# Column chunk 0 of each weight unit ahead of chunk 1, second halves evicted behind the Strassen products, third units gathered

## The chip, the cores and the metric

The kernel runs on one core of a Trainium2 chip. The metric is the device time of one execution in microseconds; the time before is 2516.99 us, the median of three runs (2516.59 to 2519.99). What can be told from no change in this kernel is about 0.2%, or 5 us.

## The reference

Two layers of a decoder trunk, float32, 256 positions, model width 2048. What matters here is which products there are and in which order they depend on one another:

```
for l in range(2):
    h = rms_norm(x, mix_norm[l]);  proj = h @ w_in[l]                # q, k, v, u/v of the SGU, two sets of gate logits
    branch_a = attention(q, k, v) @ w_attn_branch[l]                 # window 128, rotary, sinks
    branch_b = chunked_sgu(gelu(uv)) @ w_sgu_branch[l]
    merged = sigmoid(gates_a) * branch_a + sigmoid(gates_b) * branch_b
    x = x + merged @ w_out[l]
    h2 = rms_norm(x, ffn_norm[l])
    x = x + (silu(h2 @ w_gate[l]) * (h2 @ w_up[l])) @ w_down[l]      # hidden width 5632
```

## The kernel before

**Jobs, units, parts.** Every weight product is a list of *jobs* (`add_job`). A job makes 1024 output columns, two *chunks* of 512 (c = 0 and 1), for both tiles of 128 positions (t = 0 and 1): four PSUM banks. There are five banks (`banks`), so a job starts with the one bank that the job before didn't use. The contraction runs over *units* of 512 rows. A unit comes in two loads of 256 rows (h = 0 and 1, 1 MB each, on SyncE's queue, four raw buffers), and each load holds two *parts* of 256 rows and 512 columns. A part is 12 matmuls: two tiles, two blocks of 128 rows, and three products, because each operand is split into a high and a low half (`three`, lines 320 to 322).

**The stream.** The parts of all jobs form one list. `Stream.fill` runs a few parts ahead of TensorE: ScalarE writes a part's high half (`high`, line 223, six buffers), VectorE its low half (`low`, line 231, five buffers). VectorE makes a low half when TensorE has released the buffer five parts earlier. While TensorE works at part n, VectorE makes the low half of part n+4, ScalarE the high half of part n+5, and VectorE the weight sum of part n+6 if it needs one (`add`, line 215).

**Strassen.** In 42 jobs the first unit goes through seven products of 6 matmuls instead of four parts (`PRODUCTS`: 11, t1, t2, 22, t3, 21, t4). Four of the seven need a weight sum (t1, t2, t3, t4). Between them ScalarE copies banks: after 11 into x, after t1 into `p5` and after t2 into `u2` (`kept`, line 345), after t3 into y (line 365). Product 22 writes the bank that `p5` was copied from, t3 the one that `u2` was copied from, t4 the bank y. After t4, VectorE adds `u2` and `p5` into the two banks of chunk 1 (lines 367 and 368). These are all jobs from the second set of gates on: two gate halves (gate0, gate1), two w_out halves, and in the FFN, which runs in three rounds of 4, 4 and 3 blocks of 512 hidden columns, the gate and up jobs and the two down halves of each round. A gate half is followed by the matching w_sgu_branch half (sgu0, sgu1), which has two units and no Strassen. In the third round the last hidden block is one job whose two chunks are gate and up.

**The order of the other work** is written by hand, by each engine's program order. `soon(fn)` issues fn in the next step, behind that step's `fill`. `after(n, fn)` issues it n *slots* later; a part is one slot, a Strassen product half a slot. When a chunk's last part is issued, `done(c, ps)` is called:

- gate jobs: tanh on ScalarE at once (lines 959, 1002), both tiles; on VectorE, `gated` (line 1007) by `soon`.
- up jobs: `upped` (line 1016) by `soon`, both tiles; one slot later the block is transposed.
- branch jobs: `gated` and `merge` (lines 968 and 981) by `soon`; one slot later the transposition.
- w_out and down: the residual add (line 915) by `soon`; where a norm follows, one slot later the transposition and two later the squares on ScalarE (line 533).

**Transposition** (`transposed`) makes a chunk into a unit for a later job. Either two VectorE block transposes (line 414), sixteen small DMAs that GpSimd issues (line 419, `gathered`), then ScalarE's high half (line 462) and VectorE's low half (line 469) when 5 slots or more have gone by; or (`on_pe`) eight transposes on TensorE (line 483) with the halves read from PSUM. The third unit of four (o = 2, or `f == fs[2]`) goes by TensorE, the others by the gather.

Before, the parts of a unit run (h, c) = (0,0), (0,1), (1,0), (1,1). Chunk 0 so ends one part before its job, and its eviction falls into the job's last part; chunk 1's falls into the next job's first step, and its transposition one slot, that is two products, later.

Of the kernel before, what the change touches and what calls it, by code (L numbers as in the profile page):

```python
# [11 lines left out]
ALU = mybir.AluOpType  # L12
AX = mybir.AxisListType

P = 128
NT = 2
# [11 lines left out]
CW = 512  # L28
NCH = D // CW
# [6 lines left out]
N_LOW = 5  # L36
N_BIG = 24
G_BUSY, G_LAND = 3.5, 1.5
Q_FIRST = 15
Q_STEP = 4  # L40
LOAD_BY = (1, 2, 3, 4)
ROUNDS = ((0, 1, 2, 3), (4, 5, 6, 7), (8, 9, 10))
M_OUT, M_FFN, M_DOWN = 1, 1, 1
# [6 lines left out]
def hybrid_trunk(ctx: ExitStack, tc: tile.TileContext, x, mix_norm, w_in, q_norm, k_norm, sinks,  # L50
# [56 lines left out]
    def add_job(cols, units=None, m=0):  # L107
        job = Job(cols, units, m)
        jobs.append(job)
        held = {}  # L110
        for u in job.units[:m]:
            held[u] = load_of(job, u, 0), load_of(job, u, 1)
        for i, name in enumerate(PRODUCTS if m else ()):
            for n, u in enumerate(job.units[:m]):
                a, b = held[u]
                v = {"11": (a, 0), "12": (a, 1), "21": (b, 0), "22": (b, 1), "new": (f"sum{len(jobs)}_{u}", 0)}
                dst, one, two = {"11": ("11", 0, 0), "22": ("22", 0, 0), "21": ("21", 0, 0),
                                 "t1": ("new", "12", "11"), "t2": ("11", "22", "new"),
                                 "t3": ("12", "22", "12"), "t4": ("new", "21", "11")}[name]
# [776 lines left out]
    def residual(units, nxt, sums, out_at=None):  # L896

        for j in range(0, NCH, 2):

            def done(c, ps, j=j):  # L900
                o = j + c
                soon(lambda: added(o, ps))
                if nxt is not None:
                    after(2 if o == 2 else 1, lambda: nxt.unit(o, on_pe=o == 2, sums=sums and o == 0))
                    after(2, lambda: nxt.squares(o))
                    if o == NCH - 1:
                        after(4, lambda: nxt.finish())

            def added(o, ps):
                for t in range(NT):  # L910
                    n = 2 if out_at is not None and o == NCH - 1 else 1
                    w = CW // n
                    for i in range(n):
                        sl = slice(o * CW + i * w, o * CW + (i + 1) * w)
                        nc.vector.tensor_tensor(out=xs[:, t, sl], in0=ps[t][:, i * w:(i + 1) * w], in1=xs[:, t, sl],  # L915
                                                op=ALU.add)
                        if out_at is not None:
                            eng = nc.sync if i == 0 else nc.scalar
                            eng.dma_start(out_at[0, t * P:(t + 1) * P, sl], xs[:, t, sl])
            run(units, done)  # L920

    prepare(0)
# [1 line left out]
    for l in range(DEPTH):  # L924

        pl = layer[l]
        parameters(pl)
        kv = slot([P, NT, CW], name="kv")
        qs = [slot([P, NT, CW], name="q") for _ in range(2)]
        att, spa = Attention(pl), Spatial(pl, norm)  # L930

        def scaled_into(dst, ps):
            for t in range(NT):
                nc.vector.tensor_scalar(out=dst[:, t, :], in0=ps[t], scalar1=norm.r[t], scalar2=None, op0=ALU.mult)

# [12 lines left out]
        for done in (kv_done, q_done)[::-1 if l else 1]:  # L948
            run(norm.units, done)
        run(norm.units, spa.v)  # L950
        run(norm.units, spa.u)

        ga, gb, mT = [None] * NCH, [None] * NCH, [None] * NCH

        def gate(dst, j):
            def done(c, ps):
                dst[j + c] = slot([P, NT, CW], name="gate")
                for t in range(NT):
                    nc.scalar.activation(dst[j + c][:, t, :], ps[t], AF.Tanh, scale=norm.rh[t])
            run(norm.units, done)  # L960

        def branch(dst, j, units, then=None):
            def done(c, ps):
                d = dst[j + c]

                def gated():
                    for t in range(NT):
                        nc.vector.scalar_tensor_tensor(out=d[:, t, :], in0=d[:, t, :], scalar=1.0, in1=ps[t],
                                                       op0=ALU.add, op1=ALU.mult)
                        if then is not None:  # L970
                            then(j + c, t)

                soon(gated)
                if then is not None:
                    after(2 if j + c == 2 else 1,
                          lambda: transposed(mT, j + c, ga[j + c], scale=0.5, on_pe=j + c == 2,
                                                sums=M_OUT and j + c == 0))
            run(units, done)

        def merge(j, t):  # L980
            nc.vector.tensor_tensor(out=ga[j][:, t, :], in0=ga[j][:, t, :], in1=gb[j][:, t, :], op=ALU.add)

        for j in (0, 2):
            gate(ga, j)
        after(2, lambda nrm=norm: nrm.add_sums(0))
        for j in (0, 2):
            branch(ga, j, att.attT)
        for j in (0, 2):
            gate(gb, j)
            branch(gb, j, spa.sguT, merge)  # L990

        norm = Norm(ffn_cols(l))
        residual(mT, norm, M_FFN)

        nxt = Norm(mix_cols(l + 1)) if l + 1 < DEPTH else None
        for i, fs in enumerate(ROUNDS):
            hid, hT = {}, {}

            def gate_done(f, ps):
                hid[f] = a = slot([P, NT, CW], name="hid")  # L1000
                for t in range(NT):
                    nc.scalar.activation(a[:, t, :], ps[t], AF.Tanh, scale=norm.rh[t])

                def gated():
                    for t in range(NT):
                        th = a[:, t, :]
                        nc.vector.scalar_tensor_tensor(out=th, in0=th, scalar=1.0, in1=ps[t], op0=ALU.add, op1=ALU.mult)

                soon(gated)

            def up_done(f, ps):
                a = hid[f]

                def upped():
                    for t in range(NT):
                        nc.vector.scalar_tensor_tensor(out=a[:, t, :], in0=ps[t], scalar=norm.rr[t], in1=a[:, t, :],
                                                       op0=ALU.mult, op1=ALU.mult)

                soon(upped)
                after(2 if f == fs[2] else 1, lambda: transposed(hT, f, a, on_pe=f == fs[2], sums=f in fs[:M_DOWN]))  # L1020

            for f in fs[::2]:
                if f + 1 < NF:
                    run(norm.units, lambda c, ps: gate_done(f + c, ps))
                    run(norm.units, lambda c, ps: up_done(f + c, ps))
                else:
                    run(norm.units, lambda c, ps: (gate_done, up_done)[c](f, ps))
# [44 lines left out]
```

## Time and profile before

| | |
|---|---|
| median of 3 runs | 2516.99 us |
| the profiled execution | 2519.38 us, its span 2517.7 us |
| TensorE busy | 2481.6 us (99%), 11102 matmuls |
| VectorE busy | 1900.4 us (75%) |
| ScalarE busy | 1344.8 us (53%) |
| GpSimd busy | 465.0 us (18%) |
| HBM read | 475.27 MB |

A row of the groups names line, engine and operation, what is written from what, the count, then busy time and the mean ns of one, then the engine's idle time before it and who ended it. A row of the timeline is start, length, engine and line. A wait row is who waited for whom, the total in us, how often, and the longest. PEld is TensorE's weight load, which runs ahead of the matmul that it belongs to. The ends of matmuls are modelled and overlap, so a stall of TensorE is read from start to start.

### The profile page before, as it was taken

How to read it: one execution, taken by the hardware profiler on the slowest of the kernel's cores; microseconds unless marked ns; L12 is line 12 of the kernel's file. 1: busy time of each engine (PE TensorE's matmuls, PEld its weight loads, DVE VectorE, ACT ScalarE, POOL GpSimd, SP SyncE). 2: the span in 40 equal slices, each digit the busy share in tenths (PEclk: the TensorE clock that was granted, in tenths of full speed). 3: DMA queues.
4: the chain of work that ended last, by engine and by line, in shares of the span. 5: the costliest groups of instructions: out<-in, count | busy, mean ns of one | idle time of the engine just before them, and what ended most of it. 6: DMA issues, size and time to landing. Idle time of an engine off the chain costs nothing. (4 is left out here: it accounts for less than half of the span.)

```text
span 2517.7 us, 30567 instructions
## 1 busy us (share of the span) xinstructions
PE 2481.6 (99%) x11102; PEld 2031.9 (81%) x11102; DVE 1900.4 (75%) x2183; ACT 1344.8 (53%) x1658; POOL 465.0 (18%) x767
## 2 busy tenths in 40 slices
PE   9999999999999999999999999999999999999999
PEld 7888887778888888888788888877788888788887
DVE  6796667787877787777868956678878776877686
ACT  5455455465554555555654544554656455645554
POOL 1512302131210021003225022021402100210020
PEclk9999999999999999999999999999999999999999
DMA  7745656656565656566666456565756656665654
GB/s 267 232 156 164 205 200 201 192 188 221 181 229 168 233 184 219 191 217 202 217 211 216 155 166 215 193 202 165 227 199 214 208 186 209 197 209 184 223 179 164
DMA packets 157271, 502.99 MB, mean 200 GB/s; under 512 B 19712, under 2 KB 22368, under 8 KB 157120
## 3 DMA queue, kind: packets, MB, share of 16 engines
q1 hardware_dynamic: 133408, 476.87, 56.9%
q0 software_dynamic: 23392, 23.89, 3.6%
q8 instruction: 87, 1.43, 0.2%
q14 instruction: 64, 0.52, 0.1%
q10 hardware_dynamic: 320, 0.27, 0.0%
HBM read 475.27 MB, written 2.10 MB: 190 GB/s over the span
## 5 line engine op out<-in xcount | busy, mean ns | idle before, releaser
L231 DVE TENSOR_TENSOR wlo<-raw,whi 128x1024 fp32r<-128x1024 f32 (+1 forms) x940 | 1131.7, 1219 | 489.9 <-PE acc L321 401.1
L223 ACT ACTIVATE whi<-raw 128x1024 fp32r<-128x1024 f32 (+1 forms) x940 | 978.6, 1058 | 824.2 <-PE acc L322 789.9
L320 PE MATMUL acc<-whi,uh 128*128 128x512 f32 x3164 | 1240.9, 392 | 7.9 <-DVE acc L367 3.6
L321 PE MATMUL acc<-wlo,uh 128*128 128x512 f32 x3164 | 1233.0, 390 | 3.0 <-DVE wlo L231 3.0
L322 PE MATMUL acc<-whi,ul 128*128 128x512 f32 x3164 | 1233.0, 390 | 0.0
L320 PEld LDWEIGHTS acc<-whi,uh 128*128 128x128 f32 x3164 | 594.5, 188 | 139.1 <-DVE acc L367 7.4
L321 PEld LDWEIGHTS acc<-wlo,uh 128*128 128x128 f32 x3164 | 594.8, 188 | 125.2 <-DVE wlo L231 3.9
L322 PEld LDWEIGHTS acc<-whi,ul 128*128 128x128 f32 x3164 | 594.6, 188 | 125.1
L419 POOL DMA_DIRECT2D tt<-blk x624 | 359.4, 583 | 1749.0 <-ACT whi L223 725.5
L320 PE MATMUL acc<-whi,sh 128*128 128x512 f32 x336 | 139.2, 414 | 19.1 <-ACT p L345 11.0
L223 ACT ACTIVATE whi<-sum 128x1024 fp32r<-128x1024 f32 x84 | 89.3, 1063 | 101.8 <-PE acc L322 58.0
L321 PE MATMUL acc<-wlo,sh 128*128 128x512 f32 x336 | 132.0, 393 | 0.0
L322 PE MATMUL acc<-whi,sl 128*128 128x512 f32 x336 | 131.9, 393 | 0.0
L231 DVE TENSOR_TENSOR wlo<-sum,whi 128x1024 fp32r<-128x1024 f32 x84 | 101.8, 1212 | 8.4 <-PE acc L321 8.4
L320 PEld LDWEIGHTS acc<-whi,sh 128*128 128x128 f32 x336 | 63.4, 189 | 52.2 <-ACT p L345 23.3
L322 PEld LDWEIGHTS acc<-whi,sl 128*128 128x128 f32 x336 | 63.4, 189 | 14.1
L469 DVE SCALAR_TENSOR_TENSOR ul<-tt,uh 128x512 fp32r<-128x512 f32 x44 | 28.4, 687 | 58.3 <-ACT uh L462 58.3
L321 PEld LDWEIGHTS acc<-wlo,sh 128*128 128x128 f32 x336 | 63.6, 189 | 10.3
L462 ACT ACTIVATE uh<-tt 128x1024 fp32r<-128x1024 f32 x22 | 23.2, 1057 | 81.1 <-DMA tt<-blk 81.1
L215 DVE TENSOR_TENSOR raw<-raw,sum 128x1024 f32<-128x1024 f32 x42 | 51.4, 1225 | 1.4
L215 DVE TENSOR_TENSOR sum<-raw 128x1024 f32<-128x1024 f32 x42 | 51.2, 1219 | 0.0
L215 DVE TENSOR_TENSOR raw<-raw,raw 128x1024 f32<-128x1024 f32 x42 | 51.2, 1218 | 0.0
(144 smaller groups left out, 1144.9 us busy)
## 6 DMA issues: line engine op xcount, KB each, us to landing
raw<-in_w_in_dram SPq DMA_DIRECT2D x112, 1024.0 KB, 5.0
raw<-in_w_down_dram SPq DMA_DIRECT2D x88, 1024.0 KB, 5.9
raw<-in_w_gate_dram SPq DMA_DIRECT2D x80, 1024.0 KB, 5.4
raw<-in_w_up_dram SPq DMA_DIRECT2D x80, 1024.0 KB, 5.2
raw<-in_w_out_dram SPq DMA_DIRECT2D x32, 1024.0 KB, 6.1
tt<-blk POOLq DMA_DIRECT2D x624, 32.0 KB, 5.2
raw<-in_w_attn_branch_dram SPq DMA_DIRECT2D x16, 1024.0 KB, 5.6
raw<-in_w_sgu_branch_dram SPq DMA_DIRECT2D x16, 1024.0 KB, 5.3
```

What stands on the lines that cost most here:

```text
L215: nc.vector.tensor_tensor(out=self.raw(dst), in0=self.raw(total[0]), in1=self.raw(total[1]), op=ALU.subtract)
L223: nc.scalar.activation(hi[:, k, :], raw[:, k, :], AF.Copy)
L231: nc.vector.tensor_tensor(out=lo[:, k, :], in0=raw[:, k, :], in1=hi[:, k, :].bitcast(F32), op=ALU.subtract)
L320: nc.tensor.matmul(ps, a, hi, start=first, stop=False, skip_group_check=True)
L321: nc.tensor.matmul(ps, a, lo, start=False, stop=False, skip_group_check=True)
L322: nc.tensor.matmul(ps, b, hi, start=False, stop=last, skip_group_check=True)
L419: nc.gpsimd.dma_start(ov[j * B:(j + 1) * B, i], blk[i * B:(i + 1) * B, j].rearrange("p k t c -> p (k t) c"))
L462: nc.scalar.activation(unit.hi[:, k0 + k:k0 + k + step, :], src_t[:, k:k + step, :], AF.Copy, scale=scaled(k0 + k))
L469: nc.vector.scalar_tensor_tensor(out=flat(unit.lo[:, kk, :]), in0=flat(src_t[:, k:k + step, :]), scalar=scaled(k0 + k), in1=flat(unit.hi[: ...
```

## The change

1. In jobs with two chunks, each unit without Strassen asks for both its loads first, and its parts run (h, c) = (0,0), (1,0), (0,1), (1,1). Chunk 0 so ends two parts before its job.
2. `evicting(c, fn, then, ahead)` sets when a chunk is evicted. Chunk 0, and everything in the last job: both tiles by `soon`, `then` one slot later. Chunk 1: tile 0 by `soon`; tile 1 three slots later if the next job begins with Strassen, else one; `then` four slots later, or else two. ScalarE's tanh (`ahead`) of chunk 1 runs at once for tile 0 and one slot before tile 1's eviction for tile 1.
3. `then` holds the merge (one instruction over both tiles, where there were two), the transposition, the residual's squares, and a slot behind them the norm's `finish`.
4. Third units go through the gather. Only the last hidden block (`f == NF - 1`) is still transposed on TensorE.

```diff
             else:
-                for h in range(2):
-                    a = load_of(job, u, h)
-                    for c in range(2):
-                        parts.append(((a, c), None, a))
+                ab = [load_of(job, u, h) for h in range(2)]
+                for c in range(2):
+                    for h in range(2):
+                        parts.append(((ab[h], c), None, ab[h]))
                         job.steps.append(("whole", u, (h, c)))
...
+T1_LATE, THEN_LATE = 3, 4
+    def behind(whole, strassen):
+        return strassen if job_no[0] < len(jobs) and jobs[job_no[0]].m else whole
+
+    def evicting(c, fn, then=None, ahead=None):
+        if c == 0 or job_no[0] == len(jobs):
+            for t in range(NT):
+                if ahead is not None:
+                    ahead(t)
+                soon(lambda t=t: fn(t))
+            if then is not None:
+                after(1, then)
+        else:
+            late = behind(1, T1_LATE)
+            if ahead is not None:
+                ahead(0)
+                after(late - 1, lambda: ahead(1))
+            soon(lambda: fn(0))
+            after(late, lambda: fn(1))
+            if then is not None:
+                after(behind(2, THEN_LATE), then)
...
 residual:
-                soon(lambda: added(o, ps))
-                if nxt is not None:
-                    after(2 if o == 2 else 1, lambda: nxt.unit(o, on_pe=o == 2, sums=sums and o == 0))
-                    after(2, lambda: nxt.squares(o))
+                def then():
+                    nxt.unit(o, sums=sums and o == 0)
+                    nxt.squares(o)
                     if o == NCH - 1:
-                        after(4, lambda: nxt.finish())
+                        after(1, lambda: nxt.finish())
+                evicting(c, lambda t: added(o, t, ps), then if nxt is not None else None)
...
 gate:
+                evicting(c, lambda t: None, ahead=tanh)
 branch:
+                def then_():
+                    then(j + c)
+                    transposed(mT, j + c, ga[j + c], scale=0.5, sums=M_OUT and j + c == 0)
+                evicting(c, lambda t: nc.vector.scalar_tensor_tensor(...),
+                         then_ if then is not None else None)
...
-        def merge(j, t):
-            nc.vector.tensor_tensor(out=ga[j][:, t, :], in0=ga[j][:, t, :], in1=gb[j][:, t, :], op=ALU.add)
+        def merge(j):
+            nc.vector.tensor_tensor(out=flat(ga[j]), in0=flat(ga[j]), in1=flat(gb[j]), op=ALU.add)
...
 FFN:
+                evicting(c, gated, ahead=tanh)
-                soon(upped)
-                after(2 if f == fs[2] else 1, lambda: transposed(hT, f, a, on_pe=f == fs[2], sums=f in fs[:M_DOWN]))
+                evicting(c, upped, lambda: transposed(hT, f, a, on_pe=f == NF - 1, sums=f in fs[:M_DOWN]))
```

More of the change, by code (lines that the diff above doesn't have):

```diff
@@ L901, in done, with added @@
                 o = j + c
-                soon(lambda: added(o, ps))
-                if nxt is not None:
-                    after(2 if o == 2 else 1, lambda: nxt.unit(o, on_pe=o == 2, sums=sums and o == 0))
-                    after(2, lambda: nxt.squares(o))
+                def then():
+                    nxt.unit(o, sums=sums and o == 0)
+                    nxt.squares(o)
                     if o == NCH - 1:
-                        after(4, lambda: nxt.finish())
[L909 to L919, printed above, removed]
+                        after(1, lambda: nxt.finish())
+                evicting(c, lambda t: added(o, t, ps), then if nxt is not None else None)
+            def added(o, t, ps):
+                n = 2 if out_at is not None and o == NCH - 1 else 1
+                w = CW // n
+                for i in range(n):
+                    sl = slice(o * CW + i * w, o * CW + (i + 1) * w)
+                    nc.vector.tensor_tensor(out=xs[:, t, sl], in0=ps[t][:, i * w:(i + 1) * w], in1=xs[:, t, sl],
+                                            op=ALU.add)
+                    if out_at is not None:
+                        eng = nc.sync if i == 0 else nc.scalar
+                        eng.dma_start(out_at[0, t * P:(t + 1) * P, sl], xs[:, t, sl])
             run(units, done)
@@ L957, in done, with tanh @@
                 dst[j + c] = slot([P, NT, CW], name="gate")
-                for t in range(NT):
+                def tanh(t):
                     nc.scalar.activation(dst[j + c][:, t, :], ps[t], AF.Tanh, scale=norm.rh[t])
+                evicting(c, lambda t: None, ahead=tanh)
             run(norm.units, done)
@@ L964, in done @@
                 d = dst[j + c]
[L966 to L977, printed above, removed]
+                def then_():
+                    then(j + c)
+                    transposed(mT, j + c, ga[j + c], scale=0.5, sums=M_OUT and j + c == 0)
+                evicting(c, lambda t: nc.vector.scalar_tensor_tensor(out=d[:, t, :], in0=d[:, t, :], scalar=1.0,
+                                                                     in1=ps[t], op0=ALU.add, op1=ALU.mult),
+                         then_ if then is not None else None)
             run(units, done)
-        def merge(j, t):
-            nc.vector.tensor_tensor(out=ga[j][:, t, :], in0=ga[j][:, t, :], in1=gb[j][:, t, :], op=ALU.add)
+        def merge(j):
+            nc.vector.tensor_tensor(out=flat(ga[j]), in0=flat(ga[j]), in1=flat(gb[j]), op=ALU.add)
         for j in (0, 2):
@@ L997, in hybrid_trunk, with gate_done, tanh, gated @@
             hid, hT = {}, {}
-            def gate_done(f, ps):
+            def gate_done(f, c, ps):
                 hid[f] = a = slot([P, NT, CW], name="hid")
-                for t in range(NT):
+                def tanh(t):
                     nc.scalar.activation(a[:, t, :], ps[t], AF.Tanh, scale=norm.rh[t])
[L1004 to L1011, printed above, removed]
-                a = hid[f]
[L1014 to L1017, printed above, removed]
-                soon(upped)
-                after(2 if f == fs[2] else 1, lambda: transposed(hT, f, a, on_pe=f == fs[2], sums=f in fs[:M_DOWN]))
+                def gated(t):
+                    th = a[:, t, :]
+                    nc.vector.scalar_tensor_tensor(out=th, in0=th, scalar=1.0, in1=ps[t], op0=ALU.add, op1=ALU.mult)
+                evicting(c, gated, ahead=tanh)
+            def up_done(f, c, ps):
+                a = hid[f]
+                def upped(t):
+                    nc.vector.scalar_tensor_tensor(out=a[:, t, :], in0=ps[t], scalar=norm.rr[t], in1=a[:, t, :],
+                                                   op0=ALU.mult, op1=ALU.mult)
+                evicting(c, upped, lambda: transposed(hT, f, a, on_pe=f == NF - 1, sums=f in fs[:M_DOWN]))
             for f in fs[::2]:
                 if f + 1 < NF:
-                    run(norm.units, lambda c, ps: gate_done(f + c, ps))
-                    run(norm.units, lambda c, ps: up_done(f + c, ps))
+                    run(norm.units, lambda c, ps: gate_done(f + c, c, ps))
+                    run(norm.units, lambda c, ps: up_done(f + c, c, ps))
                 else:
-                    run(norm.units, lambda c, ps: (gate_done, up_done)[c](f, ps))
+                    run(norm.units, lambda c, ps: (gate_done, up_done)[c](f, c, ps))
             if i == len(ROUNDS) - 1:
```

## The prediction

> **What bounds the kernel now.** I read the page first, then TensorE's waits, then the timeline of one place where TensorE stands.
>
> ```profile
> span 2517.7 us, 30567 instructions
> ...
> PE 2481.6 (99%) x11102; PEld 2031.9 (81%) x11102; DVE 1900.4 (75%) x2183; ACT 1344.8 (53%) x1658; POOL 465.0 (18%) x767
> ```
>
> TensorE is the bound. Work taken from it counts in full; otherwise only its stalls can be won. The weight loads' waits name them:
>
> ```profile
> PEld acc L320 <- ACT p L345: 23.3, 36, 2.5
> PEld acc L320 <- ACT u L345: 18.4, 39, 2.1
> PEld acc L320 <- DVE acc L367: 7.4, 13, 1.7
> PEld acc L320 <- ACT acc L365: 5.0, 5, 1.0
> ```
>
> All four belong to the Strassen products: 54.1 us in 93 waits. One of them at close range, where gate follows up (TensorE, ScalarE, VectorE, then GpSimd):
>
> ```profile
> 642.65 0.39 PE L320 MATMUL acc<-whi,uh 128*128 128x512 f32 x1
> ...
> 646.51 0.39 PE L322 MATMUL acc<-whi,sl 128*128 128x512 f32 x1
> 647.66 0.50 PE L320 MATMUL acc<-whi,sh 128*128 128x512 f32 x1 [0.77 <-ACT p L345]
> 648.00 0.40 PE L321 MATMUL acc<-wlo,sh 128*128 128x512 f32 x1
> ```
>
> ```profile
> 646.07 1.06 ACT L223 ACTIVATE whi<-sum 128x1024 fp32r<-128x1024 f32 x1 [1.27 <-DVE sum L215]
> 647.03 0.58 ACT L345 ACTIVATE p<-acc 128x512 f32<-128x512 f32 x1
> ...
> 648.46 0.59 ACT L345 ACTIVATE u<-acc 128x512 f32<-128x512 f32 x1
> ```
>
> ```profile
> 637.26 1.22 DVE L231 TENSOR_TENSOR wlo<-raw,whi 128x1024 fp32r<-128x1024 f32 x1 [1.50 <-PE acc L321]
> 638.40 1.22 DVE L215 TENSOR_TENSOR raw<-raw,raw 128x1024 f32<-128x1024 f32 x1
> 639.98 1.23 DVE L231 TENSOR_TENSOR wlo<-raw,whi 128x1024 fp32r<-128x1024 f32 x1 [0.36 <-PE acc L321]
> 641.12 1.40 DVE L1016 SCALAR_TENSOR_TENSOR hid<-acc,rr,hid 128x512 f32<-128x512 f32 x2
> 642.44 1.29 DVE L414 STREAM_TRANSPOSE blk<-hid 128x512 f32<-128x512 f32 x2
> 643.66 1.18 DVE L231 TENSOR_TENSOR wlo<-raw,whi 128x1024 fp32r<-128x1024 f32 x1
> 644.76 1.21 DVE L215 TENSOR_TENSOR sum<-raw,raw 128x1024 f32<-128x1024 f32 x1
> ```
>
> ```profile
> 644.32 1.19 POOL L419 DMA_DIRECT2D tt<-blk  x2 [71.07 <-PE acc L322]
> ```
>
> Call Z the start of the job's first product, here 642.65. The 18 matmuls of 11, t1 and t2 start 0.227 us apart (642.65 to 646.51 is 17 steps): a product is 1.36 us, a part 2.72. Product 22 was due at 646.74, Z+4.09. It started at 647.66, and its second matmul 0.34 behind its first: 0.92 and 0.11 lost, 1.03 in all. The chain runs backwards: 22 waits for the copy `p5`; ScalarE has ahead of it the high half of t4's weight sum; that waits for VectorE's sum, which ended at 645.97. Call that end A, from Z: A = 3.32. 22 starts at A+1.69, so A = 2.40 would cost nothing. A is late because chunk 0's eviction and block transposes stand ahead of the sum.
>
> **Stalls now.** A weight load's wait holds about 0.15 that is no stall (here start to start 1.03; every product's load waits a little), so the four rows are 54.1 - 93 x 0.15 = 40.2 us. A base of about 0.15 remains in each of the 42 Strassen jobs, 6.3 us.
>
> **Part by part. Transposes off TensorE.**
>
> ```profile
> 2455.62 0.87 PE pt L483 x8
> ```
>
> Nine third units leave it: two of the merge, three of norms, four of the FFN (the last hidden blocks stay). 9 x 0.87 = 7.8 us, in full. In exchange VectorE gets 1.22 each (642.44 to 643.66) and GpSimd 16 issues. The gathered third unit is first asked for at about Z and takes, by these rows (GpSimd's first issue, ScalarE's first read):
>
> ```profile
> 735.03 4.59 POOL L419 DMA_DIRECT2D tt<-blk  x8 [67.03 <-ACT u L345]
> ```
>
> ```profile
> 750.83 1.06 ACT L462 ACTIVATE uh<-tt 128x1024 fp32r<-128x1024 f32 x1 [4.74 <-DMA tt<-blk]
> ```
>
> ```profile
> 560.83 1.73 POOL L419 DMA_DIRECT2D tt<-blk  x3 [24.28 <-ACT junk L533]
> ```
>
> ```profile
> 576.33 1.71 ACT L462 ACTIVATE uh<-tt,vcols 128x256 fp32r<-128x256 f32 x4 [1.98 <-DMA tt<-blk]
> ```
>
> 15.8 and 15.5 us; I take 15.7. It is in use from Z + 7 x 1.36 + 4 x 2.72 = Z+20.4; landing, high and low half end by Z+18.5. Hidden, with 2 us to spare. The Trainium skill, "VectorE: DVE Perf Modes", section "Rules for kernel authors", speaks against this step: a 128x128 transpose belongs on TensorE if it may go to PSUM. By that rule the 7.8 us would be left where they are, and the sum be 2512. Here TensorE is the full engine, so I go by the rows.
>
> **Chunk 0 earlier.** VectorE's row of work from Z-5.39 (637.26) is then: low half and sum (2 x 1.14), eviction 1.32, transposes 1.22, two low halves (2 x 1.14), t4's sum 1.21: A = 2.92. The work before the sum is the same; it only starts where VectorE idled 0.36. So up to gate keeps 2.92 - 2.40 = 0.52 over the base. The other kinds by their own evictions:
>
> ```profile
> L915 DVE TENSOR_TENSOR xs<-acc,xs 128x512 f32<-128x512 f32 (+1 forms) x66 | 41.3, 665 | 10.4 <-PE acc L322 10.4
> ...
> L1002 ACT ACTIVATE hid<-acc,rhalf 128x512 f32<-128x512 f32 x44 | 30.2, 687 | 15.0 <-PE acc L322 14.9
> ...
> L367 DVE TENSOR_TENSOR acc<-acc,u 128x512 f32<-128x512 f32 x42 | 29.0, 690 | 0.0
> ...
> L469 DVE SCALAR_TENSOR_TENSOR ul<-tt,uh 128x512 fp32r<-128x512 f32 x44 | 28.4, 687 | 58.3 <-ACT uh L462 58.3
> ...
> L968 DVE SCALAR_TENSOR_TENSOR gate<-gate,acc 128x512 f32<-128x512 f32 x32 | 21.1, 680 | 0.0
> ```
>
> Two residual adds or two `upped` come to the same 1.3, so 0.52 stands in 15 places: up to gate (6), up to down0 (4), w_out0 to w_out1 (2), w_out1 to gate (2), down0 to down1 under the next norm (1): 7.8 us. The sgu branches have the merge as well; one instruction of 128x1024 is 1.21 by L215's row, so A = 4.17 and 1.77 stays in 4 places: 7.1 us. Where chunk 0 has no transposition, VectorE is back in step and A is 2.40.
>
> **Chunk 1 later.** The squares, the second evictions and the transposes leave the products, and with them the waits on `u2` and y (L365). The wait on L367 goes because chunk 1's banks are used two parts after t4, not one. The late tile keeps its bank; it is the one that the next job leaves alone. But each gate job of the FFN puts a tanh ahead of y's copy:
>
> ```profile
> 600.29 0.39 PE L320 MATMUL acc<-whi,uh 128*128 128x512 f32 x1
> ...
> 608.65 0.39 PE L320 MATMUL acc<-whi,uh 128*128 128x512 f32 x1
> ```
>
> ```profile
> 601.47 1.22 DVE L215 TENSOR_TENSOR sum<-raw,raw 128x1024 f32<-128x1024 f32 x1
> ```
>
> ```profile
> 605.65 2.01 ACT L223 ACTIVATE whi<-raw 128x1024 fp32r<-128x1024 f32 x2
> 607.55 0.60 ACT L365 ACTIVATE acc<-acc 128x512 f32<-128x512 f32 x1
> ```
>
> Gate to up: A = 601.47 + 1.22 - 600.29 = 2.40, as said. y's copy ends at 608.15 and t4 starts at 608.65, with 0.5 to spare, ScalarE busy without a gap. A tanh of 0.69 ahead of it costs 0.2, with the slow start 0.3. Ten gate jobs: 3.0 us, new.
>
> **The last unit.** At 8 jobs (w_out0 2, first gate 2, down0 4) chunk 1 becomes the unit that the same job needs last, from Z + 9.52 + 8 x 2.72 = Z+31.3 and its stall. VectorE reaches its transposes after A, an eviction of 0.7, six low halves (6.84), an eviction, L367 and L368 (1.38), a low half. They end at A+12.0; with the merge A+13.2. First issue 0.6 later (643.73 to 644.32), 15.7 to ScalarE.
>
> - down0: 2.92 + 12.0 + 0.6 + 15.7 = 31.2, high half 1.06: 32.3 against 31.3 + 0.7. 0.4 with the low half, x 4 = 1.6.
> - first gate: halves in quarters (1.71 for four): 31.7 against 32.0. Nothing.
> - w_out0: 4.17 + 13.2 + 16.3 (0.6 and 15.7) + 1.06 = 34.7 against 31.3 + 2.0: 1.5 with the low half, x 2 = 3.0.
>
> VectorE, in order, waits for those high halves too, and then has ten weight steps of 1.14 and what belongs to chunk 0 before the next job's t4 sum. At w_out1: 36.1 + 11.4 + 2.5 = 50.0, with Z' = 34.7 + 4 x 2.72 = 45.6: A' = 4.4, 1.5 more, x 2 = 3.0. By the same count down1 and the first up come to A' near 3.1, 0.7 more in 6 places: 4.2 us.
>
> **Loads.** A pair is now needed together: from release to need 5 parts (13.6 us) instead of 6.
>
> ```profile
> raw<-in_w_down_dram SPq DMA_DIRECT2D x88, 1024.0 KB, 5.9
> ```
>
> Two landings one after the other are 11.8. Hidden; without that cover at most 1 or 2 us at a job's start.
>
> **The clock.**
>
> ```profile
> 1652.00:1656.00 4.00, 4.00 (x11) 3.14 (x12) 3.97 (x6) 3.37 (x4) 3.53 (x7) 0.57 0.98 322
> ```
>
> In layer 1, behind the longest wait of the first row above (2.5), the granted clock fell to 0.57 for 4 us: 4 x 0.43 = 1.7 us. With 1.9 there instead it may not fall: I count half, 0.9. The Trainium skill ("TensorE: Matmul & The Clock Gate", Part 1) asks for an idle window of about 3.4 us; by that neither wait would do it and the sum be 2505; the trace disagrees.
>
> **Sum.** Stalls after: 6.3 + 7.8 + 7.1 + 3.0 + 1.6 + 3.0 + 3.0 + 4.2 = 36.0, against 40.2: 4.2 won. With 7.8 and 0.9, 12.9 us. The profiled execution took 2519.38, 2.4 above the median (1.7 around its span). From the median: 2516.99 - 12.9 = 2504.1.
>
> **Rivals.**
>
> 1. *Slower: the last unit's gather is late.* Each us beyond 15.7 costs about 8 us over the 8 jobs (the first gate after 0.4). Those gathers now run beside loads that come in pairs, and third units take two more of the 24 buffers, which by my count at down0 leaves none: a block transpose would wait for the gather ahead of it. From 18.0 us on the kernel loses 5 us: 12.9 + 5 = 17.9 over 8. At 18.0, 2522. Against it: the rows are at 15.5 and 15.8 with loads running, and GpSimd is at 18%. Chance 0.07.
> 2. *No difference.* The last unit about 1 us late, or 0.5 us more of lag at the 15 places, with the tanh as computed: 2504 + 8 = 2512 to 2516. It speaks for it that t4's sum hardly moves. Chance 0.11.
> 3. *Much faster.* If the waits behind `p5` fall to the base, 40.2 - 6.3 + 7.8 + 1.7 = 43 us, 2474. VectorE's row ahead of the sum speaks against all of it; half is 2495 to 2485. Chance 0.14.
> 4. *It doesn't do what it says*: `then` waits for something else first, so that stalls stay and only 7.8 goes: 2509. This lies within the forecast.
>
> **How the numbers follow.** The forecast, 2490 to 2511, has 0.68. Range 2488 to 2514: it takes in the late unit of 1 us and part of case 3. A measurement of this kernel can tell about 0.2%, 5 us. Faster: 0.68 and 0.14, less a little at the edge: 0.81; same 0.12; slower 0.07.
>
> **What would show it.** On L483, 72 transposes fewer. In the weight loads' waits, L367 and L365 nearly gone from where they are, `u2` down to the base, `p5` still the longest, at sgu to gate and sgu to w_out near 2 us; a new wait on y's copy in up jobs. At w_out0's last unit a wait on L462. Wrong, if `p5` falls to the base everywhere (3), or if waits on L462 or L469 exceed 10 us in all (1).

## The result, and the profile after

2509.32 us, the median of 6 runs (2507.75 to 2510.52), against 2517.64 of the kernel before beside it (6 runs, 2516.19 to 2520.28): ratio 0.9965, 95% interval 0.9952 to 0.9978. That is 8.3 us faster, where 12.9 had been forecast. The profiled execution took 2510.52 us.

The head of the page of the kernel after (engines with busy time, share and number of instructions):

```profile
span 2508.7 us, 30665 instructions
...
PE 2475.6 (99%) x11030; PEld 2021.6 (81%) x11030; DVE 1907.1 (76%) x2193; ACT 1343.6 (54%) x1652; POOL 544.8 (22%) x911
```

TensorE is still the bound, with 72 instructions fewer (11102 to 11030): the nine third units have left it. Its weight loads' waits, of the kernel after (who waited for whom: total us, how often, the longest):

```profile
PEld acc L344 <- ACT p L369: 31.7, 42, 2.0
PEld acc L344 <- ACT u L369: 8.6, 42, 0.2
PEld acc L344 <- ACT uh L486: 7.8, 6, 3.7
...
PEld acc L344 <- ACT acc L389: 3.5, 10, 0.4
PEld acc L346 <- DVE ul L493: 2.6, 6, 0.4
```

The waits on `u2` are down to the base of 0.2 (8.6, from 18.4), the ones on VectorE's add of L367 are gone. But the wait on `p5` grew from 23.3 to 31.7, and there is a new one, on the halves of a gathered unit (L486 and L493, 10.4 together). The longest of these, at w_out0 of layer 0, in the timeline of the kernel after, first VectorE, then GpSimd, ScalarE and TensorE:

```profile
477.24 1.30 DVE L438 STREAM_TRANSPOSE blk<-gate 128x512 f32<-128x512 f32 x2
...
498.09 1.29 DVE L493 SCALAR_TENSOR_TENSOR ul<-tt,uh 128x512 fp32r<-128x512 f32 x2 [7.57 <-ACT uh L486]
```

```profile
479.12 1.16 POOL L443 DMA_DIRECT2D tt<-blk  x2 [5.13 <-PE acc L346]
481.41 6.33 POOL L443 DMA_DIRECT2D tt<-blk  x11 [1.13 <-issue]
489.92 0.58 POOL L443 DMA_DIRECT2D tt<-blk  x1 [2.18 <-DMA tt<-blk]
491.55 1.16 POOL L443 DMA_DIRECT2D tt<-blk  x2 [1.05 <-DMA tt<-blk]
```

```profile
497.00 1.06 ACT L486 ACTIVATE uh<-tt 128x1024 fp32r<-128x1024 f32 x1 [9.19 <-DMA tt<-blk]
```

```profile
494.49 0.39 PE L346 MATMUL acc<-whi,ul 128*128 128x512 f32 x1
498.11 0.50 PE L344 MATMUL acc<-whi,uh 128*128 128x512 f32 x1 [3.24 <-ACT uh L486]
...
500.11 0.63 PE L344 MATMUL acc<-whi,uh 128*128 128x512 f32 x1
500.54 0.63 PE L345 MATMUL acc<-wlo,uh 128*128 128x512 f32 x1
```

The block transposes end at 478.54. GpSimd issues the sixteen DMAs until 492.71, with three pauses of 1.13, 2.18 and 1.05 us, and ScalarE reads at 497.00, 18.5 us after the transposes. TensorE stands for 3.4 us (494.49 + 0.227 to 498.11), and then its matmuls start 0.43 apart instead of 0.227: the granted clock has fallen. The same 40 us by windows (busy time of PE, PEld, DVE, ACT, POOL; then clock, DMA share, GB/s), of before:

```profile
480.00:520.00 40.00, 37.93 (x165) 30.44 (x163) 30.54 (x32) 20.69 (x28) 7.97 (x15) 1.00 0.59 195
```

and of after:

```profile
480.00:520.00 40.00, 36.56 (x152) 28.99 (x151) 28.61 (x29) 21.42 (x27) 15.83 (x28) 0.96 0.55 164
```

13 matmuls fewer in the same time. The Trainium skill ("TensorE: Matmul & The Clock Gate", Part 1) halves the clock behind an idle window of about 3.4 us that runs freely; this wait of 3.4 us and the 0.43 us agree with it, while the clock fall behind 2.5 us in the kernel before does not. The length of a wait alone doesn't decide it here: in before, the wait of layer 0 at 401.57 us is as long as the one of layer 1 (2.26 us start to start) and left the clock at 1.00, and so did one of 3.36 us in kernel 9 below.

To compare kernels I use one count: for every matmul of 512 columns that follows another, the time from start to start beyond 0.227 us, from 270 us of the span on, summed by the releaser that the profile names. Matmuls at a low clock are in it.

| kernel | us (median) | stalls, us | on `p5` | on a gathered unit |
|---|---|---|---|---|
| before | 2517.6 | 46.0 | 16.8 | 0 |
| after | 2509.3 | 44.0 | 23.4 | 10.2 |
| 1: third units on TensorE | 2506.3 | 34.5 | 10.5 | 12.1 |
| 2: `then` after 3.5 slots | 2521.9 | 55.8 | 34.0 | 4.0 |
| 4: before, new order of parts | 2505.3 | 31.4 | 12.6 | 0 |
| 5: after, old order of parts | 2529.0 | 65.3 | 41.6 | 8.9 |
| 7: 3.5 slots, gather read later | 2491.2 | 28.2 | 18.1 | 0 |
| 9: after, gather read later | 2502.5 | 38.5 | 17.5 | 11.2 |
| 10: before, order, read later | 2499.4 | 27.8 | 10.4 | 0 |
| 11: 7 with third units on TensorE | 2498.3 | 27.9 | 11.4 | 6.1 |
| 12: 7 with a later reading still | 2494.7 | 31.6 | 16.8 | 5.0 |

In before, `u2` had 10.9 more, L367 5.3 and y 4.2; in after y has 2.0. So 46.0 - 44.0 = 2.0 us of stalls were won. The transposes gave 7.2: start to start, a group of eight delays the next matmul by 0.80 us, not by the 0.87 of its row. That makes 9.2, beside 9.0 between the spans.

### The profile page after: what moved, and what is told of

It is laid out like the page before. It is cut to its first block, busy times and chain, and to the rows that moved or that the text cites. A ratio compares the mean times of both kernels' runs of the same rounds, so it can differ in the third digit from the quotient of the medians.

```text
span 2508.7 us, 30665 instructions
## 1 busy us (share of the span) xinstructions
PE 2475.6 (99%) x11030; PEld 2021.6 (81%) x11030; DVE 1907.1 (76%) x2193; ACT 1343.6 (54%) x1652; POOL 544.8 (22%) x911
## 5 line engine op out<-in xcount | busy, mean ns | idle before, releaser
L345 PE MATMUL acc<-wlo,uh 128*128 128x512 f32 x3164 | 1233.6, 390 | 3.0 <-DVE wlo L232 3.0
L443 POOL DMA_DIRECT2D tt<-blk x768 | 442.5, 584 | 1673.4 <-DVE blk L438 975.4
L345 PEld LDWEIGHTS acc<-wlo,uh 128*128 128x128 f32 x3164 | 595.2, 188 | 125.9 <-DVE wlo L232 4.3
L345 PE MATMUL acc<-wlo,sh 128*128 128x512 f32 x336 | 131.3, 391 | 0.0
L344 PEld LDWEIGHTS acc<-whi,sh 128*128 128x128 f32 x336 | 62.9, 187 | 50.7 <-ACT p L369 31.7
L493 DVE SCALAR_TENSOR_TENSOR ul<-tt,uh 128x512 fp32r<-128x512 f32 x56 | 36.2, 687 | 67.0 <-ACT uh L486 61.9
L486 ACT ACTIVATE uh<-tt 128x1024 fp32r<-128x1024 f32 x28 | 29.6, 1058 | 93.1 <-DMA tt<-blk 87.7
L345 PEld LDWEIGHTS acc<-wlo,sh 128*128 128x128 f32 x336 | 63.2, 188 | 10.3
```

The costliest lines, as they stand in the source:

```text
L344: nc.tensor.matmul(ps, a, hi, start=first, stop=False, skip_group_check=True)
L345: nc.tensor.matmul(ps, a, lo, start=False, stop=False, skip_group_check=True)
L443: nc.gpsimd.dma_start(ov[j * B:(j + 1) * B, i], blk[i * B:(i + 1) * B, j].rearrange("p k t c -> p (k t) c"))
L486: nc.scalar.activation(unit.hi[:, k0 + k:k0 + k + step, :], src_t[:, k:k + step, :], AF.Copy, scale=scaled(k0 + k))
L493: nc.vector.scalar_tensor_tensor(out=flat(unit.lo[:, kk, :]), in0=flat(src_t[:, k:k + step, :]), scalar=scaled(k0 + k), in1=flat(unit.hi[: ...
```

## The experiments

The theory after the result: the change wins by the work taken from TensorE and by the cleared products, and loses at the last units, whose gather lands later than reckoned. The rival: the gain is the order of the parts alone. Numbers 3, 6 and 8 aren't in the table: they went far off.

**1. Third units back on TensorE** (the same in three places, for `mT` and `hT` too):

```diff
-                    nxt.unit(o, sums=sums and o == 0)
+                    if o == 2:
+                        after(1, lambda: nxt.unit(o, on_pe=True))
+                    else:
+                        nxt.unit(o, sums=sums and o == 0)
```

> The changed kernel with the nine third units transposed on TensorE again, one slot after chunk 0's eviction; all else as changed. My theory: TensorE gets 72 transposes back (7.8 us), but VectorE loses their block transposes from the row ahead of t4's sum, so p5's waits fall by 0.5 us in six places (down0, first gate) and by 1.2 in two (w_out0): 5.4. Net about 2.5 us slower than the changed kernel, 2512. Rival (what the prediction said, transposes count in full): 7.8 us slower, 2517.

2506.26 us (2503.5 to 2507.98), ratio 0.995 [0.9938, 0.9963]. Not slower: about 3 us faster than after, at the edge of what the runs tell apart. The waits of this kernel:

```profile
PEld acc L344 <- ACT p L369: 18.7, 36, 2.0
PEld acc L344 <- ACT uh L486: 7.9, 2, 4.3
```

The 72 transposes cost their 7.2 us again, but `p5` gives back 13 (23.4 to 10.5 start to start). The stalls of 1.85 us at the two w_out0, of 0.59 at four down0 and of 0.8 to 1.0 at the two first gates are no longer there, 8 us in all: in these jobs the third units' block transposes stood on VectorE ahead of t4's sum. The other 5 lie in other jobs, down1 and w_out1 above all. Gathering the third units, a step that I booked as a gain of 7.8 in full, was a small loss.

**2. `then` half a slot earlier**, so that the last unit's gather starts earlier:

```diff
-T1_LATE, THEN_LATE = 3, 4
+T1_LATE, THEN_LATE = 3, 3.5
```

> The changed kernel with THEN_LATE = 3.5 for 4: chunk 1's merge, transposition and squares come one part (2.72 us) earlier, right behind t4. Nothing else differs. My theory: the waits on L486 at the last unit of w_out0 and down0, 7.8 us in the weight loads' waits, fall to about 1, and what follows from them (the next job's late sum) too: 8 to 10 us faster than the changed kernel, about 2500. Rival (VectorE is late there for other reasons, or the work now collides with t4's own steps): within 2 us of it.

The slots of a job that begins with Strassen are counted in halves for seven products and then in whole parts, so what is due at 4 runs at 4.5: in program order this moves `then` by a whole part.

2521.93 us (2518.92 to 2524.53), ratio 1.0013 [1.0004, 1.0022]: 12.6 slower than after, where 2500 was expected. The waits of this kernel:

```profile
PEld acc L344 <- ACT p L369: 42.2, 42, 2.4
...
PEld acc L344 <- ACT uh L486: 3.2, 5, 1.1
```

The wait on the unit did shrink; `p5` took more than that. Why, is seen in VectorE's timeline at down0 of the first FFN round, of after:

```profile
758.35 1.29 DVE L493 SCALAR_TENSOR_TENSOR ul<-tt,uh 128x512 fp32r<-128x512 f32 x2 [5.12 <-ACT uh L486]
759.56 1.22 DVE L232 TENSOR_TENSOR wlo<-raw,whi 128x1024 fp32r<-128x1024 f32 x1
...
771.26 1.22 DVE L216 TENSOR_TENSOR sum<-raw,raw 128x1024 f32<-128x1024 f32 x1
```

and of this kernel:

```profile
757.11 1.29 DVE L493 SCALAR_TENSOR_TENSOR ul<-tt,uh 128x512 fp32r<-128x512 f32 x2 [7.72 <-ACT uh L486]
758.32 2.35 DVE L232 TENSOR_TENSOR wlo<-raw,whi 128x1024 fp32r<-128x1024 f32 x2
...
771.16 1.22 DVE L216 TENSOR_TENSOR sum<-raw,raw 128x1024 f32<-128x1024 f32 x1
```

The unit lands 1.2 us earlier, and TensorE reaches the next job so much earlier. But the edit moved the reading of the unit too: VectorE now stands at it one weight step earlier, for 7.72 us instead of 5.12, and has two low halves left behind it instead of one. The sum of the next t4 ends at the same time as before, for a job that started earlier. The reading waits in VectorE's program order, and everything behind it is late: this is the new theory, that the places of these waits lose the time and not the transposes.

**3. `then` a slot later:**

```diff
-T1_LATE, THEN_LATE = 3, 4
+T1_LATE, THEN_LATE = 3, 5
```

> The changed kernel with THEN_LATE = 5 for 4: one part (2.72 us) later. My theory: at the 8 jobs whose last unit is chunk 1 of the job before, every us late is a us lost: 8 x 2.7 less 1 us of slack at the two first gates, 18 to 22 us slower than the changed kernel, about 2529, slower than the kernel before. Rival (the gather is not on the path but in one place): under 5 us slower.

2614.11 us (2611.95 to 2617.31), ratio 1.0382 [1.0368, 1.0396]. The direction was right; the loss against after, 105 us, is five times the 20 expected. A waits row of this kernel:

```profile
PEld acc L344 <- ACT uh L486: 52.3, 8, 9.2
```

At five slots `then` falls behind the reading of the third unit on VectorE, so that the last gather begins only when the third has landed: at one down0 the third lands at 763.45 and the next block transposes start at 765.86. Eight waits of up to 9.2 us follow, and the mean granted clock is 0.983 instead of 0.998. It fits the new theory: the wait for one gather stands ahead of the start of the next.

**4. The order alone**, in the kernel before:

```diff
-                for h in range(2):
-                    a = load_of(job, u, h)
-                    for c in range(2):
-                        parts.append(((a, c), None, a))
+                ab = [load_of(job, u, h) for h in range(2)]
+                for c in range(2):
+                    for h in range(2):
+                        parts.append(((ab[h], c), None, ab[h]))
```

> The kernel before with the order of the parts alone changed, chunk 0 ahead of chunk 1. My theory: chunk 0's eviction and transposition start one part earlier on VectorE, so A falls by 0.4 in some 11 places (4.4 us), and the waits on L367 go (5.4 us): about 9 us faster than before, 2508, as fast as the whole change. Rival (the gain comes from moving chunk 1 behind the products, the order only makes room): within 2 us of the kernel before.

2505.25 us (2502.46 to 2505.41), ratio 0.9944 [0.993, 0.9957]: 4 us faster than the whole change. The waits of this kernel (L320 and L345 are the lines of before):

```profile
PEld acc L320 <- ACT p L345: 20.6, 36, 2.1
...
PEld acc L320 <- ACT u L345: 7.0, 34, 0.2
```

The order alone brings `u2` to its base and ends the waits on L367, without a later eviction. Parts 2 and 3 of the change add nothing to that in sum: kernel 1, which has them and leaves out only the gathered third units, takes 2506.3. Start to start, they win 2.1 us on `p5`, 3.9 on the copies of x and y (7.2 to 3.3) and 2.4 on VectorE's low halves, and lose 12.1 on w_out0's last unit.

**5. The change without the order** (the diff of 4 backwards).

> The changed kernel with the old order of the parts (chunks in turn within each load); late chunk 1 and gathered third units stay. My theory, after the order alone was worth 13 us: chunk 0's eviction starts a part later, so A rises by 0.4 in some 15 places (6 us), and the waits of chunk 1's banks on L391 come back (5 us): about 2520, no faster than the kernel before. Rival (once chunk 1 is late, the order matters little): within 3 us of the changed kernel, 2509.

2529.04 us (2528.72 to 2533.8), ratio 1.0051 [1.0037, 1.0065]. Slower than before by 11 and than after by 20, and 9 more than expected; the rival at 2509 falls. A waits row of this kernel:

```profile
PEld acc L344 <- ACT p L369: 44.8, 42, 2.5
```

Parts 2 to 4 live on the slack that the order makes. L367's kind of wait, which I had expected back, stayed away; the time is on `p5`.

**6. Two queues**: 8 of the 16 DMAs of a gather issued by ScalarE.

```diff
-                nc.gpsimd.dma_start(ov[j * B:(j + 1) * B, i],
+                eng = nc.gpsimd if i < 2 else nc.scalar
+                eng.dma_start(ov[j * B:(j + 1) * B, i],
```

> The changed kernel with 8 of a gather's 16 DMAs issued by ScalarE, so that GpSimd issues 8 and not 16. My theory: from the end of the block transposes to the landing it takes 11 to 12 us and not 16 to 18, the waits on L486 and L493 at the last units go (10 us in the weight loads' rows), with them the fall of the clock in layer 0 and a part of the late sums behind them: 8 to 13 us faster than the changed kernel, about 2499. Rival (the landing is set by the shared DMA engines and not by the issue, or ScalarE's issues cost what is won): within 3 us of it.

2638.23 us (2637.31 to 2640.56), ratio 1.0482 [1.0467, 1.0496]: 129 slower than after. Neither the theory nor the rival's 3 us came, but the rival had named the engine that pays. Waits, one place in VectorE's and ScalarE's timelines, and queues and issues in the DMA view, of this kernel:

```profile
ACT whi L224 <- issue: 169.0, 22, 10.3
PEld acc L344 <- ACT acc L383: 107.1, 19, 7.1
```

```profile
400.38 1.30 DVE L438 STREAM_TRANSPOSE blk<-gate 128x512 f32<-128x512 f32 x2
```

```profile
395.74 1.07 ACT L224 ACTIVATE whi<-raw 128x1024 fp32r<-128x1024 f32 x1 [1.65 <-PE acc L346]
401.72 5.25 ACTq L444 DMA_DIRECT2D tt<-blk  x8
407.07 2.00 ACT L224 ACTIVATE whi<-raw 128x1024 fp32r<-128x1024 f32 x2 [10.27 <-issue]
408.98 0.58 ACT L383 ACTIVATE acc<-acc 128x512 f32<-128x512 f32 x1
```

```profile
q10 hardware_dynamic: 117824, 14.45, 3.5%
q0 software_dynamic: 14176, 14.44, 2.7%
...
tt<-blk ACTq DMA_DIRECT2D x384, 32.0 KB, 2.2
tt<-blk POOLq DMA_DIRECT2D x384, 32.0 KB, 1.9
```

The 10.27 us before ScalarE's next high half have two parts. From 396.81 to 401.72 ScalarE stands at its first issue until VectorE's block transposes end (401.68); then eight issues take 5.25 us, about 0.65 each, where GpSimd takes 0.58. The copy of x (L383) waits behind both. Over the 48 gathers ScalarE stands idle ahead of the first issue for 122 us in all, and issues for 264. What the theory wanted of the gather itself did come: from the end of the block transposes to the landing it takes 6.6 to 11.5 us, 6.9 in the middle, against 13.2 to 18.4 in after. For the same bytes ScalarE's queue has 8 times the packets.

**7. 3.5 slots, and the gathered halves read one slot later:**

```diff
-G_BUSY, G_LAND = 3.5, 1.5
-T1_LATE, THEN_LATE = 3, 4
+G_BUSY, G_LAND = 3.5, 2.5
+T1_LATE, THEN_LATE = 3, 3.5
```

> THEN_LATE = 3.5 as in the run that was slower, and the reading of a gather put one slot later (G_LAND 2.5 for 1.5), so that the waiting instructions stand where they stand in the changed kernel. My theory of that loss: ScalarE and VectorE stood at the gather's landing one part earlier in their order, with one more low half behind it. So the p5 waits come back from 26 us to about 16, L486 stays low, and the time is 2505 to 2509. Rival (the earlier block transposes themselves are the loss): 2520.

2491.18 us (2490.27 to 2492.73), ratio 0.9897 [0.9883, 0.991]: 26.5 faster than before, 18 than after, and 30.7 than kernel 2, from which it differs by the reading's place alone. No weight load waits for a gathered unit any more. Page, waits and VectorE's timeline of this kernel:

```profile
PE 2468.8 (99%) x11030; PEld 2022.7 (81%) x11030; DVE 1908.3 (77%) x2193; ACT 1346.9 (54%) x1652; POOL 546.6 (22%) x911
```

```profile
PEld acc L344 <- ACT p L369: 27.3, 42, 2.0
...
ACT uh L486 <- DMA tt<-blk: 86.8, 27, 5.3
```

```profile
749.12 1.29 DVE L493 SCALAR_TENSOR_TENSOR ul<-tt,uh 128x512 fp32r<-128x512 f32 x2 [1.90 <-ACT uh L486]
...
760.37 1.21 DVE L232 TENSOR_TENSOR wlo<-raw,whi 128x1024 fp32r<-128x1024 f32 x1
762.33 1.23 DVE L232 TENSOR_TENSOR wlo<-raw,whi 128x1024 fp32r<-128x1024 f32 x1 [0.75 <-PE acc L345]
```

At the same unit VectorE waits 1.90 us instead of 7.72, and before the next sum it waits for TensorE again: it has caught up. The theory of the waits' places holds, and by more than it had forecast. It had counted `p5` alone; of the 27.6 us of stalls between kernels 2 and 7, 15.9 are on `p5`, 4.0 on the unit's halves, 4.5 on the copy of x and 3.9 on a bank that VectorE's residual add (L940) released late.

**8. Order and two queues**, in the kernel before (the diffs of 4 and 6).

> The kernel before with the new order of the parts and with 8 of 16 DMAs of a gather issued by ScalarE. My theory: in this kernel the gathers are early enough for TensorE, and what they cost is VectorE's wait in order for the landing; with 5 us less of it the p5 waits fall a little: 2500 to 2504, against 2505 with the order alone. Rival (ScalarE's issues, behind the block transposes, delay its copies in the Strassen products): slower than 2507.

2769.63 us (2767.81 to 2770.8), ratio 1.1002 [1.0987, 1.1017]: again the rival. A waits row of this kernel:

```profile
PEld acc L320 <- ACT u L345: 158.3, 40, 10.4
```

Here `u2`'s copy stands behind ScalarE's wait for the block transposes and its issues, at up to 10.4 us together.

**9. After, with the later reading alone:**

```diff
-G_BUSY, G_LAND = 3.5, 1.5
+G_BUSY, G_LAND = 3.5, 2.5
```

> The kernel after with one thing changed: a gathered unit's halves are read one slot (2.72 us) later than planned in the kernel after; the second chunk's transposes stay four slots behind. Theory: what the change loses are the in-order waits of ScalarE and VectorE for the gather's landing (16 to 18 us after the transposes, read after about 5 slots, 13.6 us). Reading later alone takes most of the 18 us by which the kernel with 3.5 slots and the later reading beats the kernel after: 2491 to 2497 us, and TensorE's weight loads hardly wait for the gathered high half (under 2 us, 7.8 in the kernel after). Rival: the later reading pays only because the transposes stand half a slot earlier; alone it makes units late for the jobs that use them, 2505 us or slower.

2502.52 us (2500.88 to 2505.0), ratio 0.994 [0.9928, 0.9953]: 7 us gained of the 18, between theory and rival. A waits row of this kernel:

```profile
PEld acc L344 <- ACT uh L486: 7.7, 2, 4.1
```

`p5` fell as in kernel 7 (17.5 start to start). What it lacks is w_out0: there the unit comes too late in both layers, 3.75 and 6.49 us start to start, which is 10.2 of the 11.3 between the two kernels.

**10. Order and later reading**, in the kernel before (the diffs of 4 and 9).

> The kernel before with the new order of the parts, and the gathered halves read one slot later. Theory: in the kernel with the order alone (2505 us) the halves of the gathered units are read too early as well, so this gains too, but less, since a third of the units isn't gathered and its last units come from TensorE or earlier: 2497 to 2502 us. Rival: there the waits lie beside slack, no difference: 2504 to 2506 us. If it comes to 2491 or below, nothing of parts 2 and 3 of the change is worth anything.

2499.38 us (2496.94 to 2499.6), ratio 0.9922 [0.991, 0.9935]; as the theory said. Two settings of the kernel before, its order and the reading's place, give 18 us.

**11. Kernel 7 with the third units on TensorE** (the diffs of 1 and 7).

> The kernel with 3.5 slots and the later reading (2491 us), its third units back on TensorE (72 transposes more, one slot behind chunk 0's eviction). Theory: in the kernel after, gathering the third units cost 3 us net because their landing is waited for in order; with that wait out of the way the 0.87 us of each of nine places off TensorE is a gain at last, so this is slower than 2491 by 3 to 8 us: 2494 to 2499. Rival: the gathers of the third units also crowd GpSimd's queue and so delay the last units, which is where the loss was: 2485 to 2489.

2498.26 us (2497.6 to 2500.36), ratio 0.9923 [0.9911, 0.9936]: 7.1 slower than kernel 7, as expected, but not for the reason given. Page and waits of this kernel:

```profile
PE 2476.4 (99%) x11102; PEld 2031.3 (81%) x11102; DVE 1897.4 (76%) x2175; ACT 1347.9 (54%) x1658; POOL 463.1 (19%) x767
```

```profile
PEld acc L344 <- ACT p L369: 18.8, 36, 2.0
...
PEld acc L344 <- ACT uh L486: 3.7, 1, 3.7
```

TensorE has 7.2 us more to do start to start (7.6 in busy time, 2476.4 - 2468.8), `p5` gives back 6.7 of it, and one late unit, at w_out0 of layer 1, takes 6.1 start to start. Without that wait the two would be about 1 us apart.

**12. Kernel 7 read yet a slot later:**

```diff
-G_BUSY, G_LAND = 3.5, 2.5
+G_BUSY, G_LAND = 3.5, 3.5
```

> The kernel with 3.5 slots, its gathered halves read yet another slot later (2.5 slots becomes 3.5). Theory: ScalarE still waits 86.8 us in 27 places for landings there, up to 5.3 us; reading later takes most of it and some of the waits for the banks' copies (27.3 us): 2486 to 2490. Rival: the last unit of a job then comes too late, or the ready times push units back in the jobs' order: 2495 us or slower.

2494.71 us (2492.05 to 2499.11), ratio 0.9908 [0.9895, 0.9922]: no gain; its interval meets that of kernel 7. A waits row of this kernel:

```profile
ACT uh L486 <- DMA tt<-blk: 29.0, 22, 5.7
```

ScalarE's waits for landings fell from 86.8 to 29.0, and nothing came of it: they were beside the path by now. As the rival had it, units come late: one at w_out0 (3.0 start to start), and the low halves of two others (1.0 each).

**Open.** What separates kernels 7, 9, 11 and 12 is in good part whether the last gather of w_out0 lands in time. From the end of its block transposes to its landing it took 15.1 and 14.9 us in the two layers of kernel 7, and from 14.8 to 18.8 in the other three. In after it was 18.4 and 15.7, and 2.0 of these 2.7 us lie in GpSimd's issuing (13.6 against 11.6 from the first issue to the end of the last). Why it pauses at one place more than at another was not tried, so the ranking among these four rests partly on that. Nor was a gather of two queues tried whose second half isn't issued by an engine that the products need, though numbers 6 and 8 land it in half the time.

## Why the prediction was right, and where not

**The sum.** The sign and the range were right; of the 12.9 us, 8.3 to 9.0 came. The stalls were to fall by 4.2 and fell by 2.0; the transposes were to give 7.8 and gave 7.2; the clock was to give 0.9 and gave nothing, since the fall moved from layer 1's branch to w_out0 (matmuls 0.43 apart). That the sum came so near is in part luck. By kernel 4 the order alone is worth 12 to 13 us, and the three parts that were to bring most of the gain take about 4 of it away.

**Chunk 0 earlier** was right where it stands alone: up to gate 0.59 us start to start for 0.52 and a tenth, the sgu branches 1.85 for 1.77. `p5` in all was forecast at 22.1 above the base (7.8 + 7.1 + 3.0 + 4.2) and came to 23.4 start to start, of which 3.0 are second matmuls that the forecast has in the base. The lags behind the late units (w_out1, down1, first up) came to 3.9 where 7.2 stood.

**y's copy** behind the tanh: ten up jobs at 0.19 to 0.23, where 0.3 stood. Right.

**The last unit** is the term that was mis-sized: 1.6 + 3.0 = 4.6 forecast, 10.2 measured, 5.4 of it at w_out0 of layer 0. At the eight jobs the gather took 15.4 to 18.4 us from the block transposes, where 0.6 + 15.7 had been reckoned; the 18.4 is that w_out0, where GpSimd's issuing took 13.6 us with its pauses, and the low clock behind the wait added 1.6. At the four down0 it took 16.0 to 17.1, and the stalls came to 3.6 for 1.6. This is the mechanism of rival 1, and its sign, waits of over 10 us on these halves (7.8 + 2.6 in the weight loads), did appear; the 5.6 us beyond the forecast stayed far below the 17.9 from which the kernel would have been slower. They are more than the whole error of the sum.

**Transposes off TensorE, 7.8 in full**, is the step whose reasoning failed. The work left TensorE (7.2). But "hidden, with 2 us to spare" asked only whether TensorE gets the third unit in time. VectorE's block transposes for it stand ahead of t4's sum; their price was inside my `p5` terms, booked to the order of the parts, and by kernel 1 `p5` is 12.9 us lower without them. The rule that I weighed, the Trainium skill's "VectorE: DVE Perf Modes", "Rules for kernel authors" (a 128x128 transpose on TensorE, if PSUM will do), would have kept the third units there, at 2512 by my sum. Kernel 1 ran 2506.3: the rule held, by 3 us. In kernel 11 it did not, by 7.1, and 6.1 of that is one late unit.

**Chunk 1 later** got the credit for the cleared waits on `u2` and L367. Kernel 4 shows that the order does this alone; the late evictions, merges and transposes weren't needed for it. They win 8 us elsewhere in the products and start the last gather later, which takes that back. With the later reading in both, kernels 10 and 11 stand at 2499.4 and 2498.3: no difference again.

**What I left out.** I asked when the gathered unit is there, but not where ScalarE and VectorE stand and wait for it. Reading it a slot later is worth 30.7 us at 3.5 slots, 6.8 at 4, and 5.9 without parts 2 to 4.

## What to carry to other kernels

A read of a DMA's result holds everything behind it on its engine, so place it by the landing as measured, plus a margin, before any work is moved to start the transfer earlier. Work taken from the full engine counts in full only if what replaces it does not stand ahead of something that this engine waits for; price both in one sum. Of a change in several parts, run the simplest part alone: here the order of a loop was worth more than all four parts together.

## What the runs showed of the hardware

- In after, a gather of sixteen 32 KB DMAs from one tile to another, all issued by GpSimd, took 13.2 to 18.4 us from the end of the block transposes to its landing (48 gathers, 16.0 on average). An issue takes GpSimd 0.58 us, but it pauses for 1 to 2 us between some, by the profile for the landing of earlier ones.
- With eight of the sixteen issued by ScalarE (kernel 6) a gather landed in 6.6 to 11.5 us. An issue takes ScalarE about 0.65 us, and the eight split into 117824 packets for 14.45 MB against 14176 for 14.44 MB. The Trainium skill ("DMA: Bandwidth & Descriptors", "Rules for kernel authors") says that spreading DMAs over engines saves issue time only. Here the median from issue to landing fell too, from 5.0 us in after to 1.9 and 2.2, but the kernel lost 129 us, because ScalarE waited in its program order for the source and for its own issues.
- The granted clock fell to a half behind waits of 2.5 us (before, layer 1) and of 3.4 us (after), for 3.4 us each; the same wait of 2.5 us in layer 0 of before, and one of 3.4 us in kernel 9, left it at 1.00.
